# Who makes the low halves of the up weights: VectorE, or ScalarE and an adding transfer

## The chip, the cores and the metric

The kernel runs on one core of a Trainium2 chip. The metric is the device time in microseconds of one execution; the time before is the median of three runs. The profile is a separate execution recorded by the hardware profiler. Engines are called by the profile's names: PE is TensorE, DVE is VectorE, ACT is ScalarE, POOL is GpSimd, SP is the engine whose queue issues most transfers.

## The reference, cut to what matters

The program is a decoder trunk of two layers over 512 tokens with 1024 features. Each layer has a mixer (layer 0: a gated position mixer in chunks; layer 1: sliding-window attention), then a gated feed-forward block, then a gated per-layer embedding, each added to the residual stream. The change touches the first product of the feed-forward block:

```python
def conv_ffn(xn, w_up, conv_w, conv_b, w_down):
    S = xn.shape[1]
    h = xn @ w_up                                   # 512 x 1024 times 1024 x 5632
    hp = jnp.pad(h, ((0, 0), (CONV_WIDTH - 1, 0), (0, 0)))
    c = conv_b + sum(hp[:, t:t + S] * conv_w[t] for t in range(CONV_WIDTH))
    g, u = jnp.split(c, 2, axis=-1)
    return (jax.nn.silu(g) * u) @ w_down            # 512 x 2816 times 2816 x 1024
```

All arrays are float32. The kernel multiplies with operands rounded to a shorter format (`float32r`), and so splits each operand into a high half (its rounded value) and a low half (what the rounding left). A product is three matmuls: high by high, high by low, low by high.

## The kernel before, in words

**Tiles.** The feed-forward width of 2816 is cut into 22 columns of 128, numbered j = 0 to 21. One up tile j is the 1024 x 256 block of `w_up` that gives both the gate column and the value column j. Its product is 2 outputs x 8 blocks of the contraction x 3 matmuls = 48 matmuls (`up`, through `mm3`, lines 218 to 230). In `mm3` the order within each block is: high weights by high activations, high weights by low activations, low weights by high activations. So the low half of a tile is needed first by the tile's third matmul.

**Units.** The weights of the whole program form one list of pieces, in the order in which they are used (`plan_ffn` lines 97 to 111 and the calls from line 114 on). A piece is brought from HBM by one transfer on SP's queue into a staging buffer `wraw` (`load`, line 162; three buffers, `r0` to `r2`). A piece is cut into units; an up tile is 1 MB and is two units of 128 partitions x 1024 elements. `pump` (line 173) turns each unit into halves: ACT casts it to `wh` (line 197), and DVE subtracts `wh` from `wraw` into `wl` (line 198). There are four buffers each for `wh` and `wl` (WBUFS = 4), and `chunk` (line 208) calls `pump` for four units beyond those used next, that is for this tile and the one after it. So a unit of tile j can be cast only when PE has left the same buffer, which a unit four places earlier held.

**Stages of a feed-forward block.** The columns are taken in the parts 0 to 7, 8 to 15, 16 to 21. After the first and the second part comes a "woven" down product (`woven_add`, line 478): 16 units, each used by 24 matmuls of half width (128 x 256), so that PE goes through a unit there in about half the time of an up unit. Before each woven product the up tile that follows (j = 8 or 16) is already multiplied. The weights of the up tiles 9 and 10, and 17 and 18, are prepared while the last woven units run. The third part has an ordinary down product (`dense_add`).

**Other work in these stages.** Each up tile's outputs go through `gated` (line 547): DVE multiplies by the norm factor (line 551), ACT applies the last tap of the convolution (line 557), DVE the other two (558, 559), ACT the silu (562), DVE the product (563); ACT and DVE then split the activations. The norm factor itself is late: at tile 0 it goes through POOL, a small transfer to HBM and one back (lines 376 and 401), and only then can `gated` of tile 0 begin.

**Order.** Each engine works through its own instructions in a fixed order, which the tile framework's scheduler writes at build time; waits between engines are semaphores, set from the buffers that instructions read and write. POOL's queue of transfers holds, in these stages, only the two small norm transfers of tile 0.

Of the kernel before, what the change touches and what calls it, by code (L numbers as in the profile page):

```python
# [8 lines left out]
F32 = mybir.dt.float32  # L9
F32R = mybir.dt.float32r  # L10
AF = mybir.ActivationFunctionType
ALU = mybir.AluOpType
# [4 lines left out]
KD = D // P  # L17
# [3 lines left out]
PARTS = [(0, 8), (8, 16), (16, 22)]  # L21
WOVEN = 2
PAIRS = 4
SLOTS = 9
N = S // 2
HEADS = 16
# [24 lines left out]
def tile_yoco(ctx: ExitStack, tc: tile.TileContext, t, out: bass.AP, out_b: bass.AP):  # L51
    nc = tc.nc
# [13 lines left out]
        return mmp.tile([P, S], F32, tag="mm", name=name)  # L66


    pieces, paired, woven = [], set(), set()

    def plan(ap_, n, cols, own=None):

        if own and len(own) > 1:
            m = n // len(own)
            cuts = [(q * m, m) for q in range(len(own))]
        else:
            m = n if n <= UNIT else (n // cols + 1) // 2 * cols
            cuts = [(0, m), (m, n - m)] if m < n else [(0, n)]
        pieces.append((ap_, n, cuts, own))

    def plan_cols(w, n_chunks, kk, cols=256, k0=0):
        for c in range(n_chunks):
            plan(w[c, :, k0 * cols : (k0 + kk) * cols], kk * cols, cols)
# [6 lines left out]
    def plan_woven(w, n_chunks, k0, k1):  # L90

        for c in range(n_chunks):
            n = (k1 - k0) * P
            woven.add(len(pieces))
            pieces.append((w[c, :, k0 * 256 : k1 * 256], 2 * n, [(0, n)] * 3 + [(0, n // 2)], None))

    def plan_ffn(l):
        for i, (j0, j1) in enumerate(PARTS):
            if i == 0:
                plan_cols(t["w_up"][l], j1, KD)  # L100
            else:
                plan_cols(t["w_up"][l, j0 + 1 : j1], j1 - j0 - 1, KD)
            if i + 1 < len(PARTS):
                plan_cols(t["w_up"][l, j1 : j1 + 1], 1, KD)
            else:
                plan(t["pT"][l], 2 * S, S, own=[(mp, "m4", "m5")])
                plan_cols(t["w_pin"][l], 2, 4)
            if i < WOVEN:
                plan_woven(t["w_down"][l], 4, j0, j1)
            else:  # L110
                plan_cols(t["w_down"][l], 4, j1 - j0, k0=j0)
# [4 lines left out]
    plan_cols(t["w_u"], 4, KD)  # L116
    plan_cols(t["w_out"], 4, KD)
    plan_ffn(0)
    plan_cols(t["w_gate"][0], 4, KD)
    plan_cols(t["w_kv"][0:1], 1, KD)  # L120
# [3 lines left out]
    outs = len(pieces)  # L124
    plan_cols(t["w_o"], 4, KD)
    plan_ffn(1)
    free = [(5 + j) % SLOTS for j in range(8)]
    for c in range(2):
# [5 lines left out]
    raws, ready, splits, sums = {}, {}, {}, {}  # L134
    state = {"raw": 0, "unit": 0, "next": 0, "tags": [0, 1, 2], "turn": 4, "pt": 0, "sent": {}}
# [13 lines left out]
    def weave(i, q):  # L149


        n = pieces[i][1] // 4
        g = raws[i][:, : 4 * n].rearrange("p (k b m) -> p b k m", b=4, m=P)
        if q == 0:
            s = sums[i] = staged(f"wsum{i}")[:, : 4 * n].rearrange("p (b k m) -> p b k m", b=4, m=P)
            k = n // P
            nc.vector.tensor_add(s[:, 0::3], g[:, 1:2].to_broadcast([P, 2, k, P]), g[:, 0::3])
            nc.vector.tensor_add(s[:, 2], s[:, 3], g[:, 0])
            nc.vector.tensor_add(s[:, 1], s[:, 2], g[:, 2])
        return (g[:, 0:3:2], sums[i][:, 2:4], sums[i][:, 0:2], g[:, 3:4])[q]  # L160

    def load(upto, queue=nc.sync):
        while state["raw"] < min(upto, len(pieces)):
            j = state["raw"]
            a, m = pieces[j][:2]
            r = staged(f"wraw{j}")
            ins = queue.dma_start(r[:, :m].rearrange("p (c m) -> p c m", c=2) if j in paired else r[:, :m], a)
            for front in state["sent"].pop(j, []):
                behind(ins, front)
            raws[j] = r  # L170
            state["raw"] += 1

    def pump(upto):
        while state["unit"] < min(upto, len(units)):
            i, q, lo, n = units[state["unit"]]
            load(i + 1)
            u = state["unit"]
            own = pieces[i][3]
            if own:
                pool, *tags = own[q]  # L180
                wh, wl = (pool.tile([P, n], F32R, tag=tg, name=f"own{u}_{tg}") for tg in tags)
            else:
                wh = wp.tile([P, UNIT], F32R, tag="wh", bufs=WBUFS, name=f"wh{u}")
                wl = wp.tile([P, UNIT], F32R, tag="wl", bufs=WBUFS, name=f"wl{u}")
            if i in woven:
                src = weave(i, q)
                hi, low = (x[:, :n].rearrange("p (b k m) -> p b k m", b=src.shape[1], m=P) for x in (wh, wl))
            elif i in paired:
                whole = raws[i][:, : pieces[i][1]].rearrange("p (c k n) -> p k c n", c=2, n=256)
                src = whole[:, lo // S : (lo + n) // S]  # L190
                hi, low = (x[:, :n].rearrange("p (k c n) -> p k c n", c=2, n=256) for x in (wh, wl))
            else:
                src, hi, low = raws[i][:, lo : lo + n], wh[:, :n], wl[:, :n]
            if u == 0:
                cast = nc.vector.tensor_copy(hi, src)
            else:
                cast = nc.scalar.copy(hi, src)  # L197
            state["split"] = splits[u] = cast, nc.vector.tensor_sub(low, src, hi.bitcast(F32))  # L198
            ready[u] = (wh, wl, n)
            state["unit"] += 1  # L200

    def take():
        u = state["next"]
        pump(u + 1)
        state["next"] += 1
        return ready.pop(u)

    def chunk(cols, kk, ahead=WBUFS):

        pump(state["next"] + ahead)  # L210
        parts = []
        while len(parts) < kk:
            wh, wl, n = take()
            parts += [(wh, wl, j * cols) for j in range(n // cols)]
        assert len(parts) == kk
        return parts
# [218 lines left out]
    def couple(q, name):  # L435

        if q < SLOTS:
            return [ap.tile([P, S], F32R, tag=f"a{x}{q}", name=f"{name}{x}") for x in "hl"]
        both = mp.tile([P, 2, S], F32R, tag=f"m{q - SLOTS}", name=name)
        return [both[:, 0, :], both[:, 1, :]]  # L440

    first, second = slice(0, N), slice(N, S)
    homes = [q for q in range(SLOTS + 4) if q != SLOTS - 1]

# [33 lines left out]
    def woven_add(pairs, between):  # L478
# [5 lines left out]
        def unit():  # L484
            pump(state["next"] + WBUFS)
            return take()
# [44 lines left out]
    def ffn(l, norm, nxt):  # L531
# [4 lines left out]
        def up(j, later=False):  # L536
            parts = chunk(256, KD)
            pss = []
            for s in range(2):
                ps = psum(f"up{j}_{s}")  # L540
                mm3(ps, parts, xs, s * P)
                pss.append(ps)
                if j == 0:
                    rstds.append(norm.rstd() if s else norm.begin(rows=0, halves=False, line=True))
            return pss if later else gated(j, pss)
# [20 lines left out]
        def whole(q, j, a):  # L566
            hi, lo = couple(q, f"act{j}")
            split(a, hi, lo)
            return hi, lo
# [3 lines left out]
        for i, (j0, j1) in enumerate(PARTS):  # L573
            if i < WOVEN:
                edge = at.tile([P, PAIRS, 2, N], F32R, tag="vtl", name=f"edge{i}")
                pairs = []
# [9 lines left out]
                continue  # L586
            act = [whole(SLOTS - 1, j0, ahead)]
            act += [whole(j - j0 - 1, j, up(j)) for j in range(j0 + 1, j1)]
# [74 lines left out]
    for q, k0, k1 in FIRST:  # L663
# [12 lines left out]
        if (q, k1) == (0, KD):  # L676
# [7 lines left out]
            cast, low = state["split"]  # L684
# [62 lines left out]
    for c in range(4):  # L747
# [4 lines left out]
        for j in range(2):  # L752
# [4 lines left out]
            u = tp.tile([P, S], F32, tag="sg", name=f"u{m}")  # L757
# [10 lines left out]
            hi = ap.tile([P, S], F32R, tag=f"ah{m}", name=f"ush{m}")  # L768
            lo = ap.tile([P, S], F32R, tag=f"al{m}", name=f"usl{m}")
# [240 lines left out]
    def pair(name):  # L1010
        q = state["pt"] = (state["pt"] + 1) % 3
        if q == 2:
            return [ap.tile([P, S], F32R, tag=f"a{x}{SLOTS - 1}", name=f"{name}{x}") for x in "hl"]
        return [pts4[:, 2 * q, :], pts4[:, 2 * q + 1, :]]
# [343 lines left out]
```

## Time and profile before

| what | value |
|---|---|
| median of three runs | 1121.63 us (1121.51 to 1121.77) |
| the profiled execution | 1120.52 us |
| its span from first to last instruction | 1118.8 us |
| PE busy | 1108.8 us, 99% |
| DVE busy | 868.3 us, 78% |
| ACT busy | 568.9 us, 51% |
| POOL busy | 103.9 us, 9% |
| read from HBM | 109.02 MB |

Busy times are sums over instructions. Matmuls overlap and their ends are modelled, so PE's 99% alone does not say that PE never waits; for that the starts of successive matmuls and the view of waits are read. In a row of a timeline the first number is the start, the second the duration, both in us; a bracket at its end gives the engine's idle time before the instruction and what ended it.

### The profile page before, as it was taken

The page shows a single profiled execution, that of the slowest core. Times are in us where ns is not written, and L with a number is a line of the kernel's source. Part 1 is how long each engine was busy: PE and PEld are TensorE (multiplying, and loading weights), DVE is VectorE, ACT ScalarE, POOL GpSimd, SP SyncE. Part 2 cuts the span into 40 slices and gives each one's busy share as a digit, 9 for nine tenths or more (in the row PEclk, how much of TensorE's full clock was granted, in tenths as well). Part 3 has the DMA queues.
Part 4 walks back from the last instruction along what each step waited for, and adds up shares of the span by engine and source line. Part 5 has one row for each costly group of instructions (what it writes and reads, how often), then busy time and mean ns, then how long its engine had stood idle before and what let it go on. Part 6 is the DMA issues. An engine that isn't in the chain of part 4 may idle for free.

```text
span 1118.8 us, 14875 instructions
## 1 busy us (share of the span) xinstructions
PE 1108.8 (99%) x5691; PEld 947.1 (85%) x5691; DVE 868.3 (78%) x1374; ACT 568.9 (51%) x936; POOL 103.9 (9%) x167
## 2 busy tenths in 40 slices
PE   9999999999999999999999999999999999999997
PEld 7888888889888998888888887888898889988876
DVE  5566449999788877657988997499997898785696
ACT  5733325545444544554656776255454445445543
POOL 1100210000000000022204451100000000000210
PEclk9999999999999999999999999999999999999999
DMA  8632313223331252333134224321244212522433
GB/s 296 135 114 76 113 48 113 76 76 123 142 113 39 76 189 69 101 113 113 63 88 132 76 57 151 111 93 71 76 151 136 90 38 76 189 85 88 148 103 86
DMA packets 35624, 118.40 MB, mean 106 GB/s; under 512 B 11800, under 2 KB 17440, under 8 KB 25056
## 3 DMA queue, kind: packets, MB, share of 16 engines
q1 hardware_dynamic: 34800, 116.19, 31.8%
q0 software_dynamic: 336, 0.79, 0.4%
q8 instruction: 45, 0.74, 0.3%
q10 hardware_dynamic: 416, 0.46, 0.1%
q14 instruction: 27, 0.22, 0.1%
HBM read 109.02 MB, written 2.11 MB: 99 GB/s over the span
## 4 chain that ended last, share of the span: by engine, by line
PE 68%; DVE 20%; ACT 4%; DMA 4%; issue 3%; POOL 0%; POOLq 0%; SPq 0%; ACTq 0%; DVEq 0%
PE up L229 26%; PE d L229 7%; PE dx L229 5%; DVE wl L198 5%; PE dy L229 4%; PE gate L229 4%; PE u L229 4%; PE q L229 3%; DVE c L558 3%; DVE c L559 2%; PE o L229 2%; DVE hs L551 2%; ACT wh L197 1%; PE v L241 1%; PE v L239 1%
## 5 line engine op out<-in xcount | busy, mean ns | idle before, releaser
L198 DVE TENSOR_TENSOR wl<-wraw,wh 128x1024 fp32r<-128x1024 f32 (+2 forms) x198 | 232.8, 1177 | 83.4 <-ACT wh L197 82.1
L197 ACT CAST wh<-wraw 128x1024 fp32r<-128x1024 f32 (+2 forms) x197 | 194.1, 990 | 147.9 <-PE up L229 56.1
L229 PE MATMUL up<-nf00h,wh 128*128 128x512 f32 x352 | 137.1, 390 | 0.0
L229 PE MATMUL up<-nf10h,wh 128*128 128x512 f32 x352 | 137.0, 389 | 0.0
L229 PE MATMUL up<-nf10l,wh 128*128 128x512 f32 x352 | 137.0, 389 | 0.0
L229 PE MATMUL up<-nf00l,wh 128*128 128x512 f32 x352 | 137.0, 389 | 0.0
L229 PE MATMUL up<-nf00h,wl 128*128 128x512 f32 x352 | 136.9, 389 | 0.0
L229 PE MATMUL up<-nf10h,wl 128*128 128x512 f32 x352 | 136.9, 389 | 0.0
L557 ACT ACTIVATE c<-hs,vec 128x512 f32<-128x512 f32 x88 | 71.6, 815 | 64.4 <-DVE hs L551 62.6
L558 DVE SCALAR_TENSOR_TENSOR c<-hs,vec,c 128x511 f32<-128x511 f32 x88 | 65.5, 747 | 20.4 <-ACT c L557 20.4
L229 PEld LDWEIGHTS up<-nf10h,wh 128*128 128x128 f32 x352 | 66.1, 188 | 13.7
L229 PEld LDWEIGHTS up<-nf00h,wl 128*128 128x128 f32 x352 | 66.1, 188 | 13.7
L229 PEld LDWEIGHTS up<-nf10l,wh 128*128 128x128 f32 x352 | 66.1, 188 | 13.7
L229 PEld LDWEIGHTS up<-nf00l,wh 128*128 128x128 f32 x352 | 66.1, 188 | 13.6
L229 PEld LDWEIGHTS up<-nf00h,wh 128*128 128x128 f32 x352 | 66.1, 188 | 13.6
L229 PEld LDWEIGHTS up<-nf10h,wl 128*128 128x128 f32 x352 | 66.1, 188 | 13.5
L559 DVE SCALAR_TENSOR_TENSOR c<-hs,vec,c 128x510 f32<-128x510 f32 x88 | 65.6, 748 | 2.2
L197 ACT CAST wh<-wsum 128x1024 fp32r<-128x1024 f32 x32 | 33.7, 1052 | 35.3 <-PE dy L229 11.3
L551 DVE TENSOR_TENSOR hs<-up,nf1rstd 128x512 f32<-128x512 f32 x44 | 30.1, 686 | 21.1 <-DMA nf1rstd<-nf1line 10.5
L551 DVE TENSOR_TENSOR hs<-up,nf0rstd 128x512 f32<-128x512 f32 x44 | 30.1, 686 | 20.9 <-DMA nf0rstd<-nf0line 10.4
L198 DVE TENSOR_TENSOR wl<-wsum,wh 128x1024 fp32r<-128x1024 f32 x32 | 39.1, 1221 | 9.3 <-ACT wh L197 9.2
L562 ACT ACTIVATE a<-c 128x512 f32<-128x512 f32 x44 | 27.7, 630 | 15.9 <-DVE c L559 15.8
(519 smaller groups left out, 2661.4 us busy)
## 6 DMA issues: line engine op xcount, KB each, us to landing
wraw<-in_w_up SPq DMA_DIRECT2D x44, 1024.0 KB, 4.8
wraw<-in_w_down SPq DMA_DIRECT2D x16, 1024.0 KB, 4.8
wraw<-in_w_gate SPq DMA_DIRECT2D x8, 1024.0 KB, 5.3
wraw<-in_w_down SPq DMA_DIRECT2D x8, 768.0 KB, 4.1
wraw<-in_w_u SPq DMA_DIRECT2D x4, 1024.0 KB, 10.8
wraw<-in_w_out SPq DMA_DIRECT2D x4, 1024.0 KB, 4.7
wraw<-in_w_q SPq DMA_DIRECT2D x4, 1024.0 KB, 4.8
wraw<-in_w_o SPq DMA_DIRECT2D x4, 1024.0 KB, 4.9
```

What stands on the lines that cost most here:

```text
L197: cast = nc.scalar.copy(hi, src)
L198: state["split"] = splits[u] = cast, nc.vector.tensor_sub(low, src, hi.bitcast(F32))
L229: nc.tensor.matmul(ps, w, x, start=first and j == 0, stop=last and j == len(todo) - 1, skip_group_check=onto)
L239: nc.tensor.matmul(ps, xh[:, s], wh[:, a:b], start=st, stop=False)
L241: nc.tensor.matmul(ps, xh[:, s], wl[:, a:b], start=False, stop=en)
L551: ins = nc.vector.tensor_mul(hs, ps, rstds[1])
L557: nc.scalar.activation(c, hs, AF.Identity, bias=v("conv_b", l * 2 * NJ + col), scale=cw[2])
L558: nc.vector.scalar_tensor_tensor(c[:, 1:], hs[:, : S - 1], cw[1], c[:, 1:], op0=ALU.mult, op1=ALU.add)
L559: nc.vector.scalar_tensor_tensor(c[:, 2:], hs[:, : S - 2], cw[0], c[:, 2:], op0=ALU.mult, op1=ALU.add)
L562: nc.scalar.activation(a, cs[0], AF.Silu)
```

## The change

For every up tile from j = 4 on, in both layers (18 tiles a layer, 36 tiles, 72 units), DVE's subtraction is replaced. ACT, which already casts the unit into `wh`, reads `wraw` a second time and writes its negative into `wl`, rounded to the same format: minus the high half. Then a transfer on POOL's queue reads the same unit of the weights from HBM once more and adds it to `wl` in place (`accum_op=ALU.add`), which leaves weight minus high half. PE's matmuls with `wl` now wait for that transfer to land. Tiles 0 to 3, the down weights and all other weights keep the subtraction. In the changed kernel the helpers' line numbers are some lines higher.

```diff
+ADDED = 4
...
+    def plan_up(l, j0, j1):
+
+        for j in range(j0, j1):
+            if j >= ADDED:
+                summed.add(len(pieces))
+            plan_cols(t["w_up"][l, j : j + 1], 1, KD)
+
     def plan_ffn(l):
         for i, (j0, j1) in enumerate(PARTS):
             if i == 0:
-                plan_cols(t["w_up"][l], j1, KD)
+                plan_up(l, 0, j1)
             else:
-                plan_cols(t["w_up"][l, j0 + 1 : j1], j1 - j0 - 1, KD)
+                plan_up(l, j0 + 1, j1)
             if i + 1 < len(PARTS):
-                plan_cols(t["w_up"][l, j1 : j1 + 1], 1, KD)
+                plan_up(l, j1, j1 + 1)
...
-            state["split"] = splits[u] = cast, nc.vector.tensor_sub(low, src, hi.bitcast(F32))
+            if i in summed:
+                nc.scalar.activation(low, src, AF.Copy, scale=-1.0)
+                rest = nc.gpsimd.dma_start(low, pieces[i][0][:, lo : lo + n].bitcast(F32R), accum_op=ALU.add)
+            else:
+                rest = nc.vector.tensor_sub(low, src, hi.bitcast(F32))
+            state["split"] = splits[u] = cast, rest
```

The scheduler's order differs little otherwise: ACT's 72 new instructions stand mostly right behind their casts (here and there one other ACT instruction lies between), POOL's 72 transfers stand behind the norm transfers of tile 0 with nothing else among them, and at the end of each woven product seven of its `dy` matmuls move ahead of a group of `dx`, and the first two matmuls of the next up tile move ahead of the last group of woven ones, so that the third matmul of the tile, the first that needs `wl`, has the same matmuls before it as it had.

More of the change, by code (lines that the diff above doesn't have):

```diff
@@ L66, in psum @@
         return mmp.tile([P, S], F32, tag="mm", name=name)
-    pieces, paired, woven = [], set(), set()
+    pieces, paired, woven, summed = [], set(), set(), set()
     def plan(ap_, n, cols, own=None):
```

## The prediction

> **What bounds the kernel now.** I read the page's head first, then PE's waits, then the chain that ended last, then the timelines of ACT and PE at the up tiles.
>
> ```profile
> span 1118.8 us, 14875 instructions
> PE 1108.8 (99%) x5691; PEld 947.1 (85%) x5691; DVE 868.3 (78%) x1374; ACT 568.9 (51%) x936; POOL 103.9 (9%) x167
> q1 hardware_dynamic: 34800, 116.19, 31.8%
> PE 68%; DVE 20%; ACT 4%; DMA 4%; issue 3%; POOL 0%; POOLq 0%; SPq 0%; ACTq 0%; DVEq 0%
> ```
>
> ```profile
> PE idle L278 <- DVE minus_half L281: 1.1, 1, 1.1
> PE np1ms L361 <- DVE np1quarter L352: 0.5, 1, 0.5
> PE dy L229 <- DVE h L513: 0.4, 1, 0.4
> PE sc L981 <- PE sc L982: 0.2, 1, 0.2
> ```
>
> ```profile
> 273.08 2.88 PE dy L229 x24
> 283.25 87.07 PE up L229 x384
> 1107.07 6.32 issue
> ```
>
> The second fence is all that PE waited for: 2.2 us in the whole run, of which 1.1 at the start and 0.5 in the last stage. The third says the same another way: its second row is eight up tiles, 384 matmuls, which ran without a break at 87.07 / 384 = 0.2267 us each, 10.88 us a tile. DVE's 20% of the chain is therefore no time that PE lost: where PE never idles, the chain can be followed through DVE's work that just keeps up. The kernel is bound by PE's stream of matmuls. What DVE saves is worth nothing unless PE waits for it; what makes PE wait counts in full. So the question is how long before its use each `wl` is ready.
>
> The casts of six places and one ordinary tile, on ACT (in order: tile 4, 9, 11, 17 of layer 0; 4, 9, 17 of layer 1; each the tile's first unit):
>
> ```profile
> 182.99 1.04 ACT L197 CAST wh<-wraw 128x1024 fp32r<-128x1024 f32 x1
> 277.31 1.05 ACT L197 CAST wh<-wraw 128x1024 fp32r<-128x1024 f32 x1 [2.26 <-PE dx L229]
> 291.30 1.05 ACT L197 CAST wh<-wraw 128x1024 fp32r<-128x1024 f32 x1 [1.00 <-PE up L229]
> 405.24 1.05 ACT L197 CAST wh<-wraw 128x1024 fp32r<-128x1024 f32 x1 [2.20 <-PE dx L229]
> 739.49 1.04 ACT L197 CAST wh<-wraw 128x1024 fp32r<-128x1024 f32 x1
> 834.09 1.05 ACT L197 CAST wh<-wraw 128x1024 fp32r<-128x1024 f32 x1 [2.26 <-PE dx L229]
> 962.01 1.05 ACT L197 CAST wh<-wraw 128x1024 fp32r<-128x1024 f32 x1 [2.20 <-PE dx L229]
> ```
>
> And the matmul on PE that first reads that unit's low half, in the same order:
>
> ```profile
> 188.13 0.39 PE L229 MATMUL up<-nf00h,wl 128*128 128x512 f32 x1
> 283.56 0.39 PE L229 MATMUL up<-nf00h,wl 128*128 128x512 f32 x1
> 305.33 0.39 PE L229 MATMUL up<-nf00h,wl 128*128 128x512 f32 x1
> 411.49 0.39 PE L229 MATMUL up<-nf00h,wl 128*128 128x512 f32 x1
> 744.52 0.39 PE L229 MATMUL up<-nf10h,wl 128*128 128x512 f32 x1
> 840.34 0.39 PE L229 MATMUL up<-nf10h,wl 128*128 128x512 f32 x1
> 968.26 0.39 PE L229 MATMUL up<-nf10h,wl 128*128 128x512 f32 x1
> ```
>
> Tile 11, an ordinary tile, has 305.33 - 292.35 = 13.0 us from the end of the cast to the use. Six tiles have far less: 4.1 and 4.0 us at tile 4 (188.13 - 184.03, 744.52 - 740.53), 5.2 us at tiles 9 and 17 of both layers (283.56 - 278.36 and its likes). Tile 4 is short since `gated` still lags from the late norm factor:
>
> ```profile
> 164.95 1.29 DVE L551 TENSOR_TENSOR hs<-up,nf0rstd 128x512 f32<-128x512 f32 x2 [10.36 <-DMA nf0rstd<-nf0line]
> ```
>
> Tiles 9 and 17 are short because a unit's buffer comes free four units earlier, and these units are of the woven product, which PE passes in 2.88 us (24 matmuls of half width, the `dy` row above).
>
> **The change, part by part.**
>
> ```profile
> L198 DVE TENSOR_TENSOR wl<-wraw,wh 128x1024 fp32r<-128x1024 f32 (+2 forms) x198 | 232.8, 1177 | 83.4 <-ACT wh L197 82.1 <-PE sc L982 0.4
> L562 ACT ACTIVATE a<-c 128x512 f32<-128x512 f32 x44 | 27.7, 630 | 15.9 <-DVE c L559 15.8
> wraw<-in_w_up SPq DMA_DIRECT2D x44, 1024.0 KB, 4.8
> wraw<-in_w_pin SPq DMA_DIRECT2D x4, 512.0 KB, 3.4
> out<-hm SPq DMA_DIRECT2D x2, 256.0 KB, 3.1
> nf0rstd<-nf0line POOLq DMA_DIRECT2D x1, 256.0 KB, 3.7
> n0rstd<-n0line POOLq DMA_DIRECT2D x1, 256.0 KB, 6.1
> n0line<-n0rt POOLq DMA_DIRECT2D x1, 2.0 KB, 8.8
> ```
>
> *Removed: 72 subtractions on DVE*, 72 x 1.18 = 85 us of its 868. PE waited 0.4 us for DVE in the stages concerned, so this gains between 0 and 0.4 us. I take 0. ACT's order holds `gated` too, so ACT's added work eats what DVE gains in the lag after tile 0.
>
> *Added: 72 negations on ACT.* None is in the trace. The nearest rows: a 128x512 ACTIVATE without per-partition operands takes 630 ns, half of the casts' 1.05 us for 128x1024; so 1.05 us each, 76 us in all. ACT goes from 51% to 58% busy. In an ordinary tile that lies beside PE's work. What waits behind a negation on ACT is the next cast (5.2 us ahead of its use or more) and the `gated` operations, for which PE has the eight PSUM banks, two a tile, as a cushion. In the six short places the negation is in the path of its own unit: slack 4.10 - 1.05 = 3.05 and 2.94 us at tile 4, 5.20 - 1.05 = 4.15 us at each of the other four. The tile's second unit is prepared some 2.4 us later and needed 12 matmuls = 2.72 us later, so it has about the same slack and rides on the first one's stall.
>
> *Added: 72 transfers on POOL's queue, 512 KB each, 38 MB more from HBM.* Call L the time from the end of the negation to PE's seeing the sum landed. POOL has nothing else then, so no queue is in front of it. No adding transfer is in the trace. From below: the quickest row of that queue, 3.7 us for a plain 256 KB. From above: that queue's slowest, 8.8 us. Between them, built up: 3.7 us; 256 to 512 KB plain, half of what 512 KB more cost on SP's queue (4.8 - 3.4 = 1.4), 0.7; the adding reads its own destination as well, another 512 KB, 1.4. L = 5.8 us when nothing else moves. At tiles 9 and 17 the load of a later up tile is in flight just then:
>
> ```profile
> 282.73 1.05 ACT L197 CAST wh<-wraw 128x1024 fp32r<-128x1024 f32 x1 [1.95 <-DMA wraw<-in_w_up]
> ```
>
> so another 1.4 us for sharing, L = 7.2 us.
>
> **The sum.** Tile 4: (5.8 - 3.05) + (5.8 - 2.94) = 5.6 us. Tiles 9 and 17, both layers: 4 x (7.2 - 4.15) = 12.2 us. An ordinary tile has 13.0 - 1.05 = 11.9 us, and waits for nothing. After the stall at tile 4 everything that feeds tile 5 has the same stall more time, so tiles 5 to 8 follow without another. Together 17.8, say 17.5 us. Against the profiled execution's own 1120.52 us (span 1118.8 plus 1.7 around it) that gives 1138.0; the median of the runs stands 1.1 us above that execution, so 1139 us. With L = 3.7 throughout only tile 4 stalls, 1.4 us: 1123. With L = 8.8 it is 6 x 8.8 - 22.6 = 30 us: 1152.
>
> The Trainium skill, "DMA: Bandwidth & Descriptors", section on the anatomy of a transfer on GpSimd's path, fits one as about 2.0 us plus its bytes at 436 GB/s. For 512 KB that is an estimate of 3.2 us, and of 4.4 us if the bytes are counted twice; then the six stalls would add up to under 4 us, and the time to about 1125. For 256 KB it would give 2.6 us where the rows above have 3.7 to 6.1, so the trace speaks for more than the page's fit, and the sum stays with the rows.
>
> **Rivals.**
>
> *The landing is in time (no change).* Up to L = 4.1 us tiles 9 and 17 wait for nothing and tile 4 costs at most 1.05 + 1.16 = 2.2 us in both layers together: 1121.6 to 1123.8. For it: POOL's queue is empty and PE asks for nothing else. Against: 3.7 us is the quickest row of that queue at half the size and without the adding.
>
> *The 16 DMA engines become the bound (much slower).* q1's row says 116.19 MB took 31.8% of the span, 3.06 us of all engines per MB; a 1 MB load is 3.2 us, a plain 512 KB 1.6. If adding doubles it, a tile needs 3.2 + 2 x 3.2 = 9.6 of its 10.88 us. The point from which this decides is an adding transfer that holds all engines longer than (10.88 - 3.2) / 2 = 3.84 us, 2.4 times a plain one. At three times, 4.8 us, each tile runs 2.0 us over; of 36 tiles, two in each of the six runs of up tiles are covered by the slack, so 24 x 2.0 = 47 us, and the six stalls grow by 1.6 us each: 1120 + 17.5 + 47 + 10, about 1195. For it: the 88% at only twice the price. Against: no row shows such a transfer to be slow. The Trainium skill, same page, section "Issuing engines are not separate DMA queues", holds that transfers from any engine's queue interleave on the same 16 engines; by that a second queue opens no second road, and this rival stands. No run here shows it yet.
>
> *Faster.* The mechanism would be DVE: with 85 us less on it, whatever PE loses to DVE comes back. PE is not busy for 1118.8 - 1108.8 = 10.0 us, of which 6.3 are the "issue" at the end and 1.1 the start; if all the other 2.6 were DVE's doing the time would be 1119.0. It decides only if L stays below 2.94 us as well. Against it: the constant 0.2267 us over 384 matmuls.
>
> **How the numbers follow.** 0.2% of the time, 2.2 us, is about what a measurement of this kernel can tell from no change. Chances: six stalls, as summed, 0.63, with a range of its own from 1125 to 1152; landing in time, or nearly (L below 4.1), 0.08; the DMA engines as the bound 0.20, from 1152 to 1230; faster 0.04; slower in another way, such as ACT's order holding up `gated` until PE lacks free PSUM banks, 0.05, from 1127 to 1160. So faster 0.04, same 0.08, slower 0.88. The range keeps all of the first case and about half of the DMA case: 1124 to 1190.
>
> **What the profile after would show.** PE's waits should list a DMA `wl<-in_w_up`, six times with 2 to 4 us each, at tiles 4, 9 and 17, and nothing at tiles 10 to 16. ACT's new ACTIVATE `wl<-wraw` should be near 1.05 us, DVE's busy time near 783, ACT's near 645. The issue rows should give `wl<-in_w_up` on POOL's queue x72 with 5.5 to 7.5 us to landing. The prediction is wrong if that landing is under 4 us (no stalls) or over 9 us, or if stalls stand in ordinary tiles, which would be the DMA engines' bound.

## The result and the profile after

The changed kernel takes 1166.09 us (median of four runs, 1163.64 to 1167.88) against 1121.59: a ratio of 1.0395, 95% interval 1.0376 to 1.0414, 44.5 us slower. Forecast were 1139 us and a range from 1124 to 1190. The direction was right; the loss was two and a half times the forecast one.

The page of the changed kernel, its head, its software queue and its new rows (columns as in the page before):

```profile
span 1161.9 us, 15099 instructions
PE 1124.2 (97%) x5691; PEld 954.9 (82%) x5691; DVE 787.9 (68%) x1302; ACT 633.7 (55%) x1008; POOL 167.9 (14%) x239
q1 hardware_dynamic: 34800, 116.19, 31.2%
q0 software_dynamic: 10704, 38.55, 18.0%
L207 ACT ACTIVATE wl<-wraw 128x1024 fp32r<-128x1024 f32 x72 | 75.6, 1051 | 0.0
wraw<-in_w_up SPq DMA_DIRECT2D x44, 1024.0 KB, 6.1
wl<-in_w_up POOLq DMA_DIRECT2D x72, 512.0 KB, 7.1
```

DVE lost 80 us of busy time, ACT gained 65, and a negation took the 1.05 us that had been assumed. The new transfers landed 7.1 us after issue in the median, and SP's loads of the up weights now take 6.1 us where they took 4.8.

PE's waits in the changed kernel (total us, times, longest):

```profile
PE up L242 <- DMA wl<-in_w_up: 27.7, 12, 3.8
PE idle L291 <- DVE minus_half L294: 1.1, 1, 1.1
PE tr L1035 <- DVE prs L1020: 0.2, 1, 0.2
```

The new line has twelve waits, not six. They stand at tiles 4, 9 and 17 of both layers, two at each: one for each unit. Tile 4 of layer 0 shows the pattern: the first fence has its two negations on ACT, the second the issues of its two transfers on POOL, the third PE around the waits (start, duration):

```profile
184.57 1.05 ACT L207 ACTIVATE wl<-wraw 128x1024 fp32r<-128x1024 f32 x1
...
186.99 1.05 ACT L207 ACTIVATE wl<-wraw 128x1024 fp32r<-128x1024 f32 x1
```

```profile
185.93 0.93 POOL L208 DMA_DIRECT2D wl<-in_w_up  x1 [23.51 <-DVE hs L564]
188.34 0.87 POOL L208 DMA_DIRECT2D wl<-in_w_up  x1 [1.48 <-ACT wl L207]
```

```profile
187.92 0.39 PE L242 MATMUL up<-nf00h,wh 128*128 128x512 f32 x1
188.15 0.39 PE L242 MATMUL up<-nf00l,wh 128*128 128x512 f32 x1
191.33 0.50 PE L242 MATMUL up<-nf00h,wl 128*128 128x512 f32 x1 [2.80 <-DMA wl<-in_w_up]
...
193.50 0.63 PE L242 MATMUL up<-nf00h,wl 128*128 128x512 f32 x1
193.92 0.63 PE L242 MATMUL up<-nf00h,wh 128*128 128x512 f32 x1
...
195.54 0.39 PE L242 MATMUL up<-nf00l,wh 128*128 128x512 f32 x1
198.62 0.62 PE L242 MATMUL up<-nf00h,wl 128*128 128x512 f32 x1 [2.69 <-DMA wl<-in_w_up]
199.03 0.63 PE L242 MATMUL up<-nf00h,wh 128*128 128x512 f32 x1
...
202.02 0.51 PE L242 MATMUL up<-nf00l,wh 128*128 128x512 f32 x1
202.36 0.39 PE L242 MATMUL up<-nf00h,wl 128*128 128x512 f32 x1
202.59 0.39 PE L242 MATMUL up<-nf00h,wh 128*128 128x512 f32 x1
```

The first unit's negation ended at 185.62 and PE used its sum at 191.33, 5.7 us later. The second's ended at 188.04 and was used at 198.62, 10.6 us later. Without waits the second would have been used 14 matmuls after the tile's start, at 187.92 + 3.17 = 191.09, so it came 7.5 us late. Between and after the waits many successive matmuls start 0.42 us apart (193.50, 193.92), in place of 0.227; these are called slow matmuls below.

The same readings at all six places (the last column is the tile's length beyond 10.88 us, at tiles 9 and 17 without the 1.44 us of the woven group that stands inside it):

| place | first unit: negation to use | second unit: negation to use | second use late by | tile longer by |
|---|---|---|---|---|
| layer 0, tile 4 | 5.7 | 10.6 | 7.5 | 9.3 |
| layer 0, tile 9 | 5.9 | 10.6 | 5.7 | 7.3 |
| layer 0, tile 17 | 7.6 | 11.2 | 6.3 | 6.6 |
| layer 1, tile 4 | 5.7 | 9.9 | 6.1 | 6.3 |
| layer 1, tile 9 | 6.6 | 10.2 | 5.3 | 7.0 |
| layer 1, tile 17 | 7.4 | 11.1 | 6.2 | 6.3 |

The last column sums to 42.8 us, against spans that differ by 1161.9 - 1118.8 = 43.1. So the whole loss stands in these six tiles. Lateness of the second unit makes 37.1 of it, slow matmuls after the second landing the other 5.7. Every other tile from 5 on ran in 10.88 or 10.89 us.

The views by windows of the changed kernel over two of the places and the tiles behind them (window; length; busy us and count of PE, PEld, DVE, ACT, POOL; granted clock; share of the DMA engines; GB/s), and the queues over 185 to 205 us and then 283 to 303 us:

```profile
187.90:208.10 20.20, 14.72 (x50) 11.19 (x49) 12.94 (x21) 12.36 (x18) 3.07 (x4) 0.83 0.91 206
208.10:240.70 32.60, 32.60 (x146) 27.00 (x145) 22.87 (x35) 19.55 (x26) 4.67 (x6) 1.00 0.75 162
291.10:310.80 19.70, 14.46 (x63) 11.57 (x62) 4.17 (x6) 7.83 (x11) 2.59 (x3) 0.91 0.82 210
```

```profile
q0 software_dynamic: 459, 1.68, 47.5%
q1 hardware_dynamic: 253, 1.94, 33.0%
```

```profile
q1 hardware_dynamic: 535, 3.99, 54.8%
q0 software_dynamic: 356, 1.33, 36.3%
```

The clock was granted at 0.83 and 0.91 of full speed in the two tiles with waits, and fully in the three tiles behind the first of them. The DMA engines were 80 to 91% taken there, by both queues: nearly full for these 20 us, though not over the run.

The order of the transfers shows more than the share. The second negation is the last to read its staging buffer, and 0.03 us after its end SP's queue issued the load of a later up tile, ahead of the second transfer, which POOL issued at 188.34. The row on SP, and the queues over 187.6 to 190.4, then 191.0 to 193.5, then 194.6 to 197.0 us:

```profile
188.07 0.33 SPq L175 DMA_DIRECT2D wraw<-in_w_up  x1
```

```profile
q0 software_dynamic: 123, 0.50, 100.6%
```

```profile
q1 hardware_dynamic: 76, 0.62, 89.4%
```

```profile
q0 software_dynamic: 112, 0.43, 89.3%
q1 hardware_dynamic: 16, 0.04, 4.9%
```

So at this tile the engines moved the first transfer, then the load, then the second transfer, with little overlap. At all six places such a load was issued 0.26 or 0.27 us ahead of the second transfer.

### The profile page after: what moved, and what is told of

Its sections match the earlier page's. It is cut to its first block, busy times and chain, and to the rows that moved or that the text cites. A ratio compares the mean times of both kernels' runs of the same rounds, so it can differ in the third digit from the quotient of the medians.

```text
span 1161.9 us, 15099 instructions
## 1 busy us (share of the span) xinstructions
PE 1124.2 (97%) x5691; PEld 954.9 (82%) x5691; DVE 787.9 (68%) x1302; ACT 633.7 (55%) x1008; POOL 167.9 (14%) x239
## 4 chain that ended last, share of the span: by engine, by line
PE 62%; issue 22%; DMA 7%; DVE 5%; ACT 1%; POOL 1%; SPq 0%; POOLq 0%; ACTq 0%; DVEq 0%
PE up L242 28%; PE d L242 8%; DMA wl<-in_w_up 5%; PE gate L242 4%; PE u L242 4%; PE q L242 3%; PE o L242 3%; DVE wl L210 1%; PE v L254 1%; PE pin L242 1%; DMA wraw<-in_w_v 1%; PE k L242 1%; PE v L252 1%; PE v L253 1%; PE gt L252 1%
## 5 line engine op out<-in xcount | busy, mean ns | idle before, releaser
L210 DVE TENSOR_TENSOR wl<-wraw,wh 128x1024 fp32r<-128x1024 f32 (+2 forms) x126 | 145.0, 1154 | 65.6 <-ACT wh L205 64.2
L242 PE MATMUL up<-nf00h,wl 128*128 128x512 f32 x352 | 141.0, 401 | 14.0 <-DMA wl<-in_w_up 14.0
L242 PE MATMUL up<-nf10h,wl 128*128 128x512 f32 x352 | 139.6, 397 | 13.6 <-DMA wl<-in_w_up 13.6
L208 POOL DMA_DIRECT2D wl<-in_w_up x72 | 62.5, 869 | 552.7 <-ACT wl L207 263.2
L242 PE MATMUL up<-nf00h,wh 128*128 128x512 f32 x352 | 140.1, 398 | 0.0
L242 PE MATMUL up<-nf00l,wh 128*128 128x512 f32 x352 | 139.7, 397 | 0.0
L207 ACT ACTIVATE wl<-wraw 128x1024 fp32r<-128x1024 f32 x72 | 75.6, 1051 | 0.0
```

The lines of the kernel that those rows point to most:

```text
L207: nc.scalar.activation(low, src, AF.Copy, scale=-1.0)
L208: rest = nc.gpsimd.dma_start(low, pieces[i][0][:, lo : lo + n].bitcast(F32R), accum_op=ALU.add)
L210: rest = nc.vector.tensor_sub(low, src, hi.bitcast(F32))
L242: nc.tensor.matmul(ps, w, x, start=first and j == 0, stop=last and j == len(todo) - 1, skip_group_check=onto)
```

## The experiments

The times before in the runs' own comparisons were 1122.5 to 1122.8 us.

**Only the ordinary tiles.**

```diff
-            if j >= ADDED:
+            if j in (11, 12, 13, 14, 15, 16, 19, 20, 21):
```

> Adding transfers only for the up tiles 11 to 16 and 19 to 21 of both layers (18 tiles, 36 transfers), which have 11.5 us or more from negation to use; all others keep the subtraction. Theory 1 (only the six short places, tiles 4, 9 and 17, cost anything): no wait of PE for wl, 1121.6 +-1.5 us, the same as before. Theory 2 (every transfer costs something, by its share of the DMA engines, by the negations on ACT or by a lower clock of PE): half the transfers keep about half of the 44.5 us, 1135 to 1145.

Measured: 1120.73 us, ratio 0.9985 (0.9975 to 0.9994). PE has no wait for `wl`. Half of the transfers and negations cost nothing: theory 1 stands, theory 2 falls. It was run again, with eleven executions in place of ten:

> The kernel with adding transfers in the tiles 11 to 16 and 19 to 21 alone once more, with more rounds, since its first measurement stood at 0.9985 of the time before (0.9975 to 0.9994). Theory 1 (PE had nothing to win there): 0.999 to 1.001. Theory 2 (the 36 subtractions off DVE do gain some 1.8 us): 0.9975 to 0.999 again.

Measured: 1120.44 us, ratio 0.9982 (0.9973 to 0.9991). So this is a little faster than the kernel before, by about 2 us, less than the 0.2% that had been set as the bound. Where these 2 us come from is not settled. The time before differs between the sets of runs by 1.1 us itself (1121.59 and 1122.68), and the profiled execution of this kernel has the same span as the profile before, which is of another set, 1118.8 us; it shows nothing that PE gained.

**Only the short places, and all but them.**

```diff
-            if j >= ADDED:
+            if j in (4, 9, 17):
```

> Adding transfers for the tiles 4, 9 and 17 of both layers alone (12 of the 72). Theory 1 (the six short places make the whole loss): PE waits at the same six places, with second landings somewhat earlier since no transfers of neighbouring tiles are on the way, 8.5 to 10.5 us from the negation: 3.6 to 5.6 us at each place plus about 1 us of slow matmuls, 1149 to 1162. Theory 2 (the loss grows with the number of transfers): a sixth of 44.5 us, 1129 or less.

Measured: 1168.01 us, ratio 1.0409 (1.0386 to 1.0432). Twelve transfers make the whole loss. PE's waits:

```profile
PE up L242 <- DMA wl<-in_w_up: 28.3, 12, 4.2
```

The expectation was too low: second landings took 10.2 to 11.6 us with no transfer of a neighbouring tile on the way, about what they took in the changed kernel (9.9 to 11.2), so those neighbours do not matter.

```diff
-            if j >= ADDED:
+            if j >= ADDED and j not in (9, 17) and j != 4:
```

> Adding transfers for all tiles from 4 on but 4, 9 and 17 (60 of the 72). Theory 1: the next tile after the norm factor's lag, tile 5, is now the short one (its cast ended 6.0 us before its use, of which the negation and the silu ahead of it take 2 to 3), and PE waits there 3 to 7 us a layer; tiles 10 and 18, 9.4 us and more from negation to use, wait for nothing or little: 1128 to 1137. Theory 2 (the transfers cost by their number): five sixths of 44.5 us, 1155 or more.

Measured: 1133.36 us, ratio 1.0100 (1.0082 to 1.0119), as theory 1 had it. Sixty transfers cost a quarter of what twelve did:

```profile
PE up L242 <- DMA wl<-in_w_up: 9.7, 5, 2.9
```

Four of the five waits are at tile 5, which is now the first to come with a lag behind the norm factor, and one at tile 18.

**The negations alone.**

```diff
                 nc.scalar.activation(low, src, AF.Copy, scale=-1.0)
-                rest = nc.gpsimd.dma_start(low, ..., accum_op=ALU.add)
```

> All 72 negations, none of the adding transfers: the low halves of these tiles stay minus the high half, the addition of the weights is left out. It prices ACT's new work and the removed subtractions by themselves. Theory 1 (the landing of the transfer is what costs): 1121.6 +-1.5 us, no wait of PE for wl over 0.5 us. Theory 2 (ACT's 76 us more hold up gated and the casts): 1126 or more, with PE waiting for ACT at tiles 4 to 8.

Measured: 1127.32 us, ratio 1.0047 (1.0030 to 1.0064). Neither theory had it quite: the 5 us of the second are there, but at the start of the first woven product of each layer, and PE waits there for DVE. PE's waits, the row on PE, and DVE's wait for ACT, before and in this kernel:

```profile
PE dy L241 <- DVE h L525: 5.4, 2, 2.7
```

```profile
250.78 0.38 PE L241 MATMUL dy<-act_0h,wh 128*128 128x256 f32 x1 [2.73 <-DVE h L525]
```

```profile
DVE c L558 <- ACT c L557: 20.4, 30, 0.9
```

```profile
DVE c L570 <- ACT c L569: 66.7, 54, 3.7
```

DVE waited 20.4 us for ACT's part of the convolution before, 66.7 us here. By these rows the lag after tile 0's late norm factor now shrinks at the pace of ACT, not DVE, and is not worked off when the woven product begins. In the changed kernel itself this cost does not show: PE's own stall at tile 4 gives `gated` the time, and PE has no wait at the woven products.

**One unit of each tile.**

```diff
-            if i in summed:
+            if i in summed and q == 0:
```

> From tile 4 on only the first unit of each tile gets the negation and the adding transfer, the second keeps DVE's subtraction (36 transfers). Theory 1 (at a short place the second unit's landing decides, and it is late because it shares the way with the first): the late second landing is gone and the first one's remains, 1.6 to 3.1 us at each of six places: 1121.6 + 15 to 19, so 1136 to 1141. Theory 2 (the first landing decides, the second only rides on it): the loss stays near the 44.5 us, 1160 or more.

Measured: 1144.07 us, ratio 1.0193 (1.0172 to 1.0213). The first landings alone make about the forecast's sum: the waits come to 14.6 us at six places, and slow matmuls behind two of them (3.0 us each) put the time 3 us over the expected range.

```diff
-            if i in summed:
+            if i in summed and q == 1:
```

> From tile 4 on only the second unit of each tile gets the negation and the adding transfer, the first keeps DVE's subtraction. It tells what makes the second landing late (9.9 to 11.2 us from negation to use where the first took 5.7 to 7.6). If it is the first adding transfer in front of it: landing after 6 to 7.5 us, a loss of 1 to 4 us a place, 1132 to 1140. If it is the loads on SP's queue beside it: landing still after 9 to 10.5 us, 1150 to 1160.

Measured: 1152.17 us, ratio 1.0265 (1.0244 to 1.0286), inside the range for the loads as the cause. But PE's waits make only 21.0 us of it, and some 9 us are slow matmuls behind them, which neither range counted. Landings took 8.0 to 8.9 us, mean 8.4, between the two theories: 2.2 us less than the mean of 10.6 with a first transfer in front. Here at tile 4 of layer 0:

```profile
186.84 1.05 ACT L207 ACTIVATE wl<-wraw 128x1024 fp32r<-128x1024 f32 x1
```

```profile
196.10 0.79 PE L242 MATMUL up<-nf00h,wl 128*128 128x512 f32 x1 [5.04 <-DMA wl<-in_w_up]
```

**Small loads beside the transfers.** The loads on SP's queue are cut to an eighth.

```diff
+            if j in summed:
+                ins = queue.dma_start(r[:, : m // 8], a[:, : m // 8])
+            else:
...
+                if i in summed:
+                    src = raws[i][:, lo // 8 : (lo + n) // 8].rearrange("p (o c) -> p o c", o=1).to_broadcast([P, 8, n // 8])
...
```

> The changed kernel with the loads of the up tiles from 4 on, on SP's queue, cut to an eighth (128 KB in place of 1 MB; ACT reads these columns eight times over, so the high halves of these tiles repeat and the rest of the weights is left out). The adding transfers stay as they are. Theory 1 (the loads beside it make the second landing late: alone in its tile it still took 8.0 to 8.9 us): landings of 5 to 6 us for the first and 6 to 8 us for the second, 1135 to 1145. Theory 2 (the two adding transfers hold each other up, the loads do little): second landings stay near 10 us, 1158 or more.

Measured: 1143.29 us, ratio 1.0185 (1.0165 to 1.0206), as theory 1 had it. (The expectation is wrong in one thing: no weights are left out. The adding transfer brings all of them, so the low halves make up what the repeated high halves lack.) PE's waits:

```profile
PE up L248 <- DMA wl<-in_w_up: 10.9, 8, 2.4
PE up L248 <- ACT edge L475: 3.1, 1, 3.1
```

PE still waited for the first unit at all six places, 1.2 to 3.1 us each (the second row is tile 4 of layer 0; it names an ACT instruction, but in the changed kernel the same matmul started before that instruction had ended, so this wait is counted as one for the transfer). It waited for the second unit at two places only, 0.7 us or less: these two landings took 7.1 and 7.3 us, and the other four had come before their use. One more wait, 1.1 us, stands at tile 6 of layer 1. There a load of down weights, which kept its 1 MB, was issued 0.27 us ahead of the tile's second transfer, and PE used that transfer's sum 8.55 us after the negation: late again, where a whole load stood in front. So of the second landing's 10.6 us some 3 are the load that goes ahead of it, and some 2 the first transfer in front of it (by the kernel with the second unit alone). No run held that load back behind the second transfer.

**A plain transfer.**

```diff
-                rest = nc.gpsimd.dma_start(low, ..., accum_op=ALU.add)
+                rest = nc.gpsimd.dma_start(low, ...)
```

> The transfer copies the weights over the negative high half instead of adding to it (the low half of these tiles is then the whole weight, so the addition is left out); everything else as in the changed kernel, 72 transfers of 512 KB on the same queue. Theory 1 (the adding, which reads its own destination too, is a good part of a landing: an adding transfer held all DMA engines 2.9 us against some 1.6 for a plain one): first landings 4.4 us, second ones 7 to 8 us from the negation, 1135 to 1148. Theory 2 (the queue's fixed time and the loads beside it are what a landing costs, the adding is free): 1162 to 1167.

Measured: 1152.67 us, ratio 1.0269 (1.0243 to 1.0295), between the theories. First landings took 3.9 to 5.8 us (mean 4.7, against 6.5 with the adding), second ones 6.8 to 9.0 (mean 8.1, against 10.6). With the shorter stall at tile 4 of layer 0, PE waited 1.5 us at tile 5 as well. The queue and the issue in this kernel:

```profile
q0 software_dynamic: 10704, 38.55, 10.7%
wl<-in_w_up POOLq DMA_DIRECT2D x72, 512.0 KB, 5.4
```

Less the 0.4% that other transfers of this queue took before, a plain transfer holds all 16 engines (123.4 - 4.5) / 72 = 1.65 us, an adding one (209.1 - 4.5) / 72 = 2.84 us, 1.7 times as long. So the adding itself is a quarter to a third of the loss (the two executions took 1150.39 and 1154.94 us); the rest is there with a plain transfer of the same bytes between the cast and the use.

**PE kept busy in the waits.** At tiles 4, 9 and 17, twice:

```diff
+                    if k in (0, 4):
+                        for _ in range(10):
+                            nc.tensor.matmul(other, ones, wide, start=True, stop=True, skip_group_check=True)
                     nc.tensor.matmul(pss[0], low, xh, start=False, stop=k == KD - 1)
```

> The changed kernel with 20 matmuls of constants added at each of the tiles 4, 9 and 17, ten ahead of the first matmul that needs the first unit's low half and ten ahead of the second's, into a bank that is cleared afterwards: 20 x 0.2267 = 4.5 us of work in the 5.3 to 7.5 us that PE loses there. Theory 1 (PE's clock falls because it idles, and the slow matmuls after the second landing, 5.7 us over the six places, come on top of the wait): granted clock near 1.00 at the six places, 1166 - 5.7 = 1160, no higher. Theory 2 (the clock falls for another reason, such as the transfers): clock still near 0.8 in these stretches, 1166 or more.

Measured: 1161.85 us, ratio 1.0351 (1.0330 to 1.0372). The window over tile 4 of layer 0:

```profile
187.70:207.00 19.30, 17.81 (x77) 14.09 (x76) 12.61 (x21) 10.67 (x15) 2.58 (x3) 1.00 0.90 212
```

The clock stayed at 1.00 here, with the DMA engines 90% taken as in the changed kernel, and over the whole run at 0.998 where it was 0.987. Twenty matmuls more at each of six places made the kernel 4.2 us faster (the intervals of the two ratios, 1.0330 to 1.0372 and 1.0376 to 1.0414, just fail to meet), although two new waits of 1.8 and 1.7 us came up at tile 6 of the two layers. So it was PE's idling that slowed the matmuls, not the transfers.

**Low halves last.** In the up tiles from 4 on, the 32 matmuls with `wh` for both outputs first, then the 16 with `wl`:

```diff
+            if j >= ADDED:
...
+                for s, ps in enumerate(pss):
+                    for k, ((wh, wl, off), (xh, xl)) in enumerate(zip(parts, xs)):
+                        low = wl[:, off + s * P : off + (s + 1) * P]
+                        nc.tensor.matmul(ps, low, xh, start=False, stop=k == KD - 1, skip_group_check=True)
```

> The changed kernel with another order of matmuls in the up tiles from 4 on: the 32 matmuls with the high halves of the weights for both outputs first, then the 16 with the low halves. The first low half is needed 7.3 us after the tile's start in place of 0.45, the second unit's 8.2 in place of 3.2. Theory 1 (only late landings cost): the second landings, 5.3 to 7.5 us late, have 5.0 us more, so 0.3 to 2.5 us stay at each place: 1121.6 + 7 = 1129, and up to 1135 with the lag of gated at the first woven product, 2.7 us a layer, which the run with the negations alone showed. Theory 2 (the loss is not in the landings): 1155 or more.

Measured: 1127.82 us, ratio 1.0055 (1.0038 to 1.0072), 1 us from theory 1. All 72 transfers and negations are there; only the place where PE asks for their result moved:

```profile
PE up L562 <- DMA wl<-in_w_up: 5.4, 4, 1.9
```

That took 38 of the 44.5 us away.

## Why the prediction was right or wrong

*What bounds the kernel: right.* PE had nothing to win from DVE. The subtractions gone gained no time that can be placed, and the loss is PE's waits and the slow matmuls behind them.

*Where it would wait: right.* Tiles 4, 9 and 17 of both layers, no other, though with twelve waits in place of six; in the ordinary tiles, for which 11.9 us had been reckoned, every landing came in time. The runs with the short places alone and without them settle this.

*The first landings: right.* Forecast 5.8 us at tile 4, measured 5.7 both times; forecast 7.2 at tiles 9 and 17, measured 5.9 to 7.6, mean 6.9. Forecast 17.5 us of waiting in all; the kernel with first units alone waited 14.6. Part of this is luck: the 5.8 us were 4.4 for a plain 512 KB and 1.4 for the adding, and at tile 4 the plain transfer took 3.9 us and the adding 1.8 more. The negation cost the 1.05 us that had been taken; the 630 ns row called half of a cast's 1.05 us is 0.6 of it, but the price had come from the cast.

*The second landings: wrong, and this is the step that failed.* The prediction said that the second unit "has about the same slack and rides on the first one's stall". So the sum charged one stall a place, with the first landing's 5.8 or 7.2 us, and took the second landing to be as quick. It took 9.9 to 11.2 us, 4.1 us more in the mean (10.6 against 6.5), and with the second unit late by 37.1 us in all the first wait no longer counted: it lay inside the second one. The cause is what stands in front of it on the 16 engines: the first transfer, and the load of a later up tile, which the second negation itself sets free. Around tile 4 of layer 0, in 20 us, both queues together took 80% of the engines, and 91% around tile 9. The issue row's median of 7.1 us lies in the forecast 5.5 to 7.5, and so does not show this: it is over all 72 transfers.

The prediction had reckoned the DMA engines' load over a whole tile (9.6 of 10.88 us, forecast 3.2 us a transfer, measured 2.84), found it below its limit, and not asked what two transfers and a load do that are issued within 2.5 us of each other. The Trainium skill, "DMA: Bandwidth & Descriptors", section "Issuing engines are not separate DMA queues", says that transfers from all queues run on the same 16 engines and interleave there. The runs with small loads and with the second unit alone agree that they are the same engines, with 3 us and 2 us off the second landing; but the transfers at tile 4 went one after the other more than they interleaved, as the queues' rows show. The sentence had been set beside the wrong rival: what it does here is to a latency, not to the throughput of the run.

*The clock: missing.* No term stood for it. 5.7 us of the loss are matmuls 0.42 us apart after the second landing, and keeping PE busy gave 4.2 us back. The Trainium skill, "TensorE: Matmul & The Clock Gate", Part 1, says that the array's clock falls to half after an idle window of about 3.4 us and comes back after some 3.4 us of sustained work. At tile 4 of layer 0 the return agrees: 0.42 us in place of 0.227, from 198.62 to 202.02, which is 3.4 us; other slow spells lasted from 1.7 us (where the next wait cut it off) to 6.1 us, the longest in the kernel with first units alone. The fall does not agree as stated: waits of 2.8 and 2.7 us were enough here.

*ACT at no cost: wrong in itself, hidden in the sum.* The negations alone cost 5 us at the first woven products. PSUM banks were named as the cushion for `gated`; but what ran out was the time until the woven product needs the activations. The stall at tile 4 paid for it.

*The rivals.* That every landing is in time fell with L. The DMA engines as the bound of the run fell too: 2.84 us a transfer is below the 3.84 from which that would decide, and the ordinary tiles kept 10.88 us. DVE as a gain is, at most, the unplaced 2 us of the kernel with ordinary tiles alone.

## What to carry to other kernels

Where the matmul engine hardly ever waits, taking work off another engine has next to nothing to win, and it costs where the time from "buffer free" to "first use" is shortest: list that time for every tile, not for a typical one, and for every piece of the tile. When several transfers are asked for together, the last one's landing counts. Here it came after the engines had moved what was asked for before it, a load for a later tile included; and that load was issued because the new instruction was the last to read its buffer. So ask of every instruction added which transfer its end sets free, and what that transfer then stands in front of. If a late operand can't be avoided, ask for it later: moving the matmuls that need it to the end of the tile was worth 38 us here, without a byte less to move.

## What the runs showed of the hardware that was not expected

- A 512 KB transfer from GpSimd's queue that adds to its destination held the 16 DMA engines 2.84 us, a plain one 1.65 us; first landings of a pair came 1.8 us later with the adding, second ones 2.5 us.
- A gap of a few microseconds on TensorE can cost more than itself, and not always the same: in the kernel with first units alone, starts 3.16 us apart at tile 4 of layer 0 cost 0.1 us of slow matmuls, starts 3.63 us apart at tile 4 of layer 1 cost 3.0 us. The length alone does not decide: in the kernel with second units alone, starts 2.80 us apart at tile 9 of layer 0 cost 0.2 us, starts 2.72 us apart at tile 9 of layer 1 cost 1.75 us.
- Transfers of two queues went largely one after the other: for 2.5 us at tile 4 of layer 0 the load's packets alone moved, 89% of the engines, while a transfer issued 0.27 us after it on the other queue had none.
- Twenty matmuls of constants added to each of six tiles made the kernel faster, 1161.85 us against 1166.09.
